# Neighbourhood attention on Trainium2: the position bias added by VectorE on the way out of PSUM, where TensorE had added it with identity products

## The chip, the cores and the metric

The kernel runs on one core of one Trainium2 chip. The metric is the device time of one execution in microseconds. The traces come from one profiled execution; engines are named as in the profile: PE (TensorE's matmuls) and PEld (its weight loads), DVE (VectorE), ACT (ScalarE), POOL (GpSimd), SP (SyncE, whose queue issues every DMA of this kernel).

## The reference

One step of a two-layer network over 1024 latent tokens (a grid of 16 rows of 64) and 128 context tokens of width 1024. Layer 0 mixes pooling and latent attention; layer 1 is 2-D neighbourhood attention with 16 heads of 64. Each layer ends in an MLP. The change lies in the neighbourhood attention of the latent tokens:

```python
s_loc = jnp.einsum('bqhd,bikhd->bhqik', qr, kb, ...) * scale + bias[None]
s_ctx = jnp.einsum('bqhd,blhd->bhql', qr, k_ctx, ...) * scale
s = jnp.concatenate([s_loc.reshape(B, H, GRID_W, kh * GRID_W), s_ctx], axis=-1)
p = jax.nn.softmax(s, axis=-1).astype(v.dtype)
return (jnp.einsum('bhqik,bikhd->bqhd', p_loc, vb)
        + jnp.einsum('bhql,blhd->bqhd', p_ctx, v_ctx))
```

A query sees a window of 8 rows by 16 columns. `bias` is a learned value per head and relative place, and -1e30 outside the window. Context keys have no bias.

## The kernel before, in words

The program is written with a tile library whose scheduler sets the order of the instructions of each engine; semaphores follow from it. Precision is kept by splitting operands into a high and a low half of type fp32r and summing products of halves.

The neighbourhood attention of layer 1 stands near the middle of the program, after the values' projection (`value_gen1`) and before layer 1's output projection and MLP. Tokens are ordered so that eight blocks of 128 keys each touch at most three blocks of 128 queries. A head is a generator, `na_units`, of two context units and eight key tiles:

- `scores` writes the scores of one key tile, 128 keys by 256 or 384 queries, into one of three PSUM banks (`ps_st`, tag `pa`). L1299 multiplies the high and low halves of k (`kk`) with q's high half (`qq`); L1303 multiplies `k2` with q's low half (`q2`), and a row of ones in `k2` with the negated row of maxima in `q2[64:65]`. Between the two, L1302 adds the bias: a product of the identity (`identr`) with the table of the head, once with its high half `tbh` and once with its low half `tbl`. Tiles 1 and 6 of a head take two pieces of the table, the others one: ten pieces and twenty such products a head.
- L1331 takes the exponential from the bank into `p`, and L1336 multiplies `p` with the values `nv` into `ps_pv`. The scores are transposed, keys on partitions, so `p` needs no transpose.
- Context tiles (L1312, L1314) have no bias. Sums and quotients come at the end of a half (L1003, L1004) and of a head pair (L1045 to L1049).

Beside a head, `weave` runs `na_max` for the head two later: eight times two matmuls `ps_m` (L1281, L1282; tag `pb`, three banks), then a VectorE reduction L1284 that adds the table `ta` and takes the maximum. `put_max` turns the result into a row (L1022, L1024), stores it to DRAM (`mrow`), and the load of `q2[64:65]` reads it back. For the first seven heads the context's own attention (`ctxw`, `ps_s`) runs beside them, for the last the output projection (`ps_o`).

`load_na` loads `kk`, `qq` and `ta` two heads ahead, `load_na_rest` loads `k2`, `q2`, `nv` and the table `tb` (128 x 640) one head ahead and splits `tb` with L1266 (ScalarE, `tbh`) and L1267 (VectorE, `tbl`). Most tiles come from 36 slots that are handed out oldest first (`Slots`); `tb`, `q2` and `tbh` come from the weights' rings `wr` (three buffers), `wh` and `wl` (four each). All loads go through SP's queue (L113), in order: a load that waits for a buffer holds up those behind it.

```python
for u, w, c in tabs:
    for t in (th, tlo):
        nc.tensor.matmul(ps[:, u:w], identr, t[:, c:c + w - u], start=False, stop=False)
```

Of the kernel before, what the change touches and what calls it, by code (L numbers as in the profile page):

```python
# [10 lines left out]
F32 = mybir.dt.float32  # L11
F32R = mybir.dt.float32r
AF = mybir.ActivationFunctionType
# [4 lines left out]
P = 128  # L18
# [72 lines left out]
def hybrid_kernel(ctx: ExitStack, tc: tile.TileContext, I, O):  # L91
    nc = tc.nc

    cst = ctx.enter_context(tc.tile_pool(name="cst", bufs=1))
# [5 lines left out]
    S = Slots(spool, NSLOT)  # L100
# [39 lines left out]
    vec = cst.tile([P, NVEC], F32, name="vec")  # L140
    ones = cst.tile([P, P], F32, name="ones")
    ident = cst.tile([P, P], F32, name="ident")
    identr = cst.tile([P, P], F32R, name="identr")
    sel8 = cst.tile([P, 6, 8], F32, name="sel8")
    sel8r = cst.tile([P, 6, 8], F32R, name="sel8r")
    ecnt = cst.tile([P, 4, 16], F32, name="ecnt")
# [7 lines left out]
    def W(tag, name=None):  # L154
        return wpool.tile([P, 1024], F32 if tag == "wr" else F32R, tag=tag, name=name or tag, bufs=3 if tag == "wr" else 4)
# [360 lines left out]
    dma(sel8, I["sel8"])  # L516
    dma(ecnt, I["ecnt"])
    nc.scalar.copy(sel8r, sel8)
    nc.scalar.copy(identr, ident)
    pt = PS("ps_sil", "pb")  # L520
    nc.tensor.transpose(pt[0:16, 0:P], sil, ident)
    sr = S.alloc("sr")
# [20 lines left out]
    for ch in range(NCH):  # L543
        c0 = ch * CH
        for g in range(4):
            ps = PS("ps_i")[:, :CH]
# [72 lines left out]
    for m in (2, 3, 0, 1):  # L619
        w = wtile(wsplit(I["win0"][m]))  # L620
        for ch in range(NCH):
            ps = PS("ps_i")[:, :CH]
# [83 lines left out]
    for ch in range(NCH + 1):  # L706
        cache = ch == NCH
        n = P if cache else CH
        cs = slice(0, P) if cache else slice(ch * CH, ch * CH + CH)
        ps8 = PS("ps8", "pb")[0:8, :n]  # L710
        for t in range(4):
            ps = PS("ps_k")[:, :n]
# [382 lines left out]
    rest = load_rest(0)  # L1095
    opairs = []
    for h in range(8):
# [12 lines left out]
        rest = nrest  # L1110
# [26 lines left out]
    st, h = {}, []  # L1137
# [60 lines left out]
    for g in range(4):  # L1198
# [8 lines left out]
        for t, ch in order:  # L1207
# [3 lines left out]
            ps = PS("ps_n1")[:, :CH]  # L1211
# [9 lines left out]
        for ch in range(NCH):  # L1221
            for t in range(4):
                wn = "naq" if t < 2 else "nak"
                pp_ = pq if t < 2 else pk
                ps = PS("ps_b", "pb")[:, :CH]
# [27 lines left out]
        return kk, qq, ta  # L1253

    def load_na_rest(h):
        k2, q2, v, tb = S.alloc("k2", F32R), W("wh", "q2"), S.alloc("nv"), W("wr", "tb")
        p, n0 = h // 2, 64 * (h % 2)
        rows = slice(n0, n0 + 64)
        dma(k2[0:64], kd[0][p, rows])
        dma(k2[64:65], onesr)  # L1260
        dma(q2[0:64, :NS], qd[1][p, rows])
        dma(q2[64:65, :NS], mrow1[h].rearrange("a b -> (a b)").unsqueeze(0))
        dma(tb[:, :640], I["bias_k"][h])
        load_pv(vd, h, v)
        th, tl = W("wl", "tbh"), S.alloc("tbl", F32R)
        nc.scalar.copy(th[:, :640], tb[:, :640])  # L1266
        nc.vector.tensor_sub(tl[:, :640], tb[:, :640], th[:, :640])  # L1267
        return k2, q2, v, th, tl

    mrow1 = [DR(f"mrow1{i}", [8, P]) for i in range(16)]  # L1270
    od = DR("od", [8, P, TOK], F32)
# [17 lines left out]
        yield  # L1289

    def na_units(h, tl, rest, opair, den):
        (kk, qq, _), (k2, q2, v, th, tlo) = tl, rest
        par = 64 * (h % 2)
        v3 = v.rearrange("p (t f) -> p t f", t=9)
        cp = W("wr", "cp")
        po = [None, None]

        def scores(ps, ks, qs, tabs):
            nc.tensor.matmul(ps, kk[:, ks], qq[:, qs], start=True, stop=False)  # L1299
            for u, w, c in tabs:  # L1300
                for t in (th, tlo):
                    nc.tensor.matmul(ps[:, u:w], identr, t[:, c:c + w - u], start=False, stop=False)  # L1302
            nc.tensor.matmul(ps, k2[0:65, ks], q2[0:65, qs], start=False, stop=True)  # L1303

        def close_half(half):
# [2 lines left out]
        def ctx_unit(half):  # L1308
            qs = slice(half * 512, half * 512 + 512)
            ps = PS("ps_st")  # L1310
            scores(ps, slice(0, P), qs, [])
            nc.scalar.activation(cp[:, qs], ps, AF.Exp)  # L1312
            po[half] = PS("ps_pv", "pc")
            nc.tensor.matmul(po[half], v3[:, 8, :], cp[:, qs], start=True, stop=False)  # L1314
# [4 lines left out]
        for i in range(8):  # L1319
# [6 lines left out]
            n = b - a  # L1326
            p_ = held[:, cnt * CH:cnt * CH + n]
            ps = PS("ps_st")[:, :n]
            tabs = {0: [(0, 256, 128)], 1: [(0, 128, 384), (128, 384, 128)], 6: [(0, 256, 0), (256, 384, 512)]}
            scores(ps, slice(P + i * P, 2 * P + i * P), slice(a, b), tabs.get(i, [(0, n, 0)]))  # L1330
            nc.scalar.activation(p_, ps, AF.Exp)  # L1331
            for half in range(2):
                u, w = max(a, half * 512), min(b, half * 512 + 512)
                if u >= w:
# [77 lines left out]
    for h in range(16):  # L1412
# [23 lines left out]
            of = out_first(1, acts)  # L1436
            gs.append((chain(iter([None] * OW), islice(of, OA)), OW + OA))
        weave(*gs)
        S.free(*tls[h][:2], rest[0], rest[2], rest[4])
        rest = nrest  # L1440
    run(islice(of, OB))
    later(2)
# [148 lines left out]
```

## Time and profile before

| | |
|---|---|
| Time, median of 3 runs | 3052.11 us (3050.89 to 3064.39) |
| Profiled execution: its time, its span | 3059.43 us, 3057.2 us |
| TensorE, matmuls | 2950.9 us busy, 97% |
| TensorE, weight loads | 2663.1 us, 87% |
| VectorE | 2117.4 us, 69% |
| ScalarE | 1337.7 us, 44% |
| GpSimd | 315.5 us, 10% |
| Moved by DMA | 372.39 MB, 122 GB/s on average |

The profiled execution took 7.3 us more than the median; sums over its trace are made against its own 3059.43 us. Matmuls are pipelined, so a row's mean duration of one is longer than the distance from its start to the next one's start. A share of the whole span averages over stages; the stage of the change is read by itself.

### The profile page before, as it was taken

The numbers are of one execution on the slowest core, as the hardware profiler recorded it, in microseconds if no ns is written. First come the engines' busy times: TensorE is split into PE (matmuls) and PEld (weight loads), VectorE is DVE, ScalarE is ACT, GpSimd is POOL, SyncE is SP. The second block draws the span as 40 slices with busy tenths as digits, with TensorE's granted clock in tenths as the row PEclk, the third lists the DMA queues.
The fourth block names the chain that finished last, engine by engine and source line by source line (L and its number), as shares of the span: only waits on it lengthen the run. The fifth ranks groups of instructions, "written<-read, shape, count | busy, mean of one in ns | idle before, by whom it ended". The sixth has DMA issues, their size and how long they took to land.

```text
span 3057.2 us, 46985 instructions
## 1 busy us (share of the span) xinstructions
PE 2950.9 (97%) x18622; PEld 2663.1 (87%) x18622; DVE 2117.4 (69%) x3777; ACT 1337.7 (44%) x2194; POOL 315.5 (10%) x210
## 2 busy tenths in 40 slices
PE   7998999889999999999999999989989999999999
PEld 4956666689999999999988797767989999999999
DVE  5976343797768889786899522544677678777775
ACT  5364344244436544353645422434345355453433
POOL 1014000252000020000221000000021000110000
PEclk9996999999999999999999999999999999999999
DMA  6529331432323334232566346687303232332322
GB/s 233 165 69 312 81 76 50 134 105 83 97 77 96 104 126 146 88 97 84 169 206 208 112 151 176 170 198 204 115 29 93 81 100 73 121 94 87 97 77 87
DMA packets 148269, 372.39 MB, mean 122 GB/s; under 512 B 14225, under 2 KB 67073, under 8 KB 148050
## 3 DMA queue, kind: packets, MB, share of 16 engines
q1 hardware_dynamic: 148050, 369.40, 39.4%
q8 instruction: 146, 2.39, 0.3%
q14 instruction: 73, 0.60, 0.1%
HBM read 310.69 MB, written 57.47 MB: 120 GB/s over the span
## 4 chain that ended last, share of the span: by engine, by line
PE 86%; DVE 5%; DMA 5%; issue 1%; ACT 1%; POOL 1%; SPq 0%; DVEq 0%; ACTq 0%; POOLq 0%
PE ps L453 9%; PE ps L455 9%; PE ps L454 9%; PE ps L423 8%; PE ps L425 7%; PE ps L424 7%; PE ps_pv L1079 4%; PE ps_pv L1336 2%; PE ps_n L336 2%; PE ps_n L337 2%; PE ps_n L338 2%; PE ps_v L1360 1%; DVE trash L201 1%; PE ps_v L1362 1%; PE ps_v L1361 1%
## 5 line engine op out<-in xcount | busy, mean ns | idle before, releaser
L453 PE MATMUL ps<-ml,wh 128*128 128x288 f32 x2048 | 591.9, 295 | 10.1 <-DVE ml L442 7.8
L454 PE MATMUL ps<-mh,wl 128*128 128x288 f32 x2048 | 600.9, 295 | 0.0
L455 PE MATMUL ps<-mh,wh 128*128 128x288 f32 x2048 | 596.5, 295 | 0.0
L423 PE MATMUL ps<-bl,wh 128*128 128x288 f32 x1792 | 532.7, 297 | 13.4 <-DVE bl L354 10.2
L424 PE MATMUL ps<-bh,wl 128*128 128x288 f32 x1792 | 529.5, 295 | 0.0
L425 PE MATMUL ps<-bh,wh 128*128 128x288 f32 x1792 | 528.0, 295 | 0.0
L453 PEld LDWEIGHTS ps<-ml,wh 128*128 128x128 f32 x2048 | 381.3, 188 | 11.1 <-DVE ml L442 8.3
L454 PEld LDWEIGHTS ps<-mh,wl 128*128 128x128 f32 x2048 | 385.2, 188 | 0.0
L455 PEld LDWEIGHTS ps<-mh,wh 128*128 128x128 f32 x2048 | 383.3, 188 | 0.1
L459 DVE SCALAR_TENSOR_TENSOR x<-ps,ada,x 128x288 f32<-128x288 f32 (+2 forms) x640 | 269.8, 450 | 120.3 <-PE ps L455 118.8
L423 PEld LDWEIGHTS ps<-bl,wh 128*128 128x128 f32 x1792 | 336.7, 188 | 16.5 <-issue 11.5
L425 PEld LDWEIGHTS ps<-bh,wh 128*128 128x128 f32 x1792 | 338.3, 189 | 0.0
L424 PEld LDWEIGHTS ps<-bh,wl 128*128 128x128 f32 x1792 | 337.4, 188 | 0.2
L396 ACT CAST wh<-s 128x512 fp32r<-128x512 f32 x256 | 146.1, 618 | 306.9 <-PE ps L455 216.6
L161 ACT CAST wh<-wr 128x1024 fp32r<-128x1024 f32 x188 | 197.0, 1049 | 169.8 <-PE ps L425 80.1
L201 DVE CUSTOM_DVE_ANT_0 trash<-wada,silu 128x1024 bf16<-128x1024 f32 x160 | 214.5, 1340 | 17.9 <-DMA wada<-in_wada 7.6
L162 DVE TENSOR_TENSOR wl<-wr,wh 128x1024 fp32r<-128x1024 f32 x144 | 179.7, 1251 | 44.9 <-ACT wh L161 44.8
L396 ACT CAST wh<-wr 128x1024 fp32r<-128x1024 f32 (+1 forms) x128 | 106.9, 835 | 219.8 <-PE ps L455 155.5
L162 POOL TENSOR_TENSOR wl<-wr,wh 128x1024 fp32r<-128x1024 f32 x44 | 124.1, 2827 | 707.2 <-ACT wh L161 707.1
L1037 DVE TENSOR_REDUCE stat<-ps_m 128x1 f32<-128x384 f32 x192 | 98.3, 551 | 121.2 <-PE ps_m L1036 120.9
L1284 DVE CUSTOM_DVE_ANT_0 trash<-ps_m,ta 128x512 bf16<-128x512 f32 (+1 forms) x128 | 84.0, 656 | 122.0 <-PE ps_m L1282 113.4
L397 DVE TENSOR_TENSOR wl<-s,wh 128x512 fp32r<-128x512 f32 x232 | 157.6, 711 | 5.1 <-ACT wh L396 2.8
(321 smaller groups left out, 6248.9 us busy)
## 6 DMA issues: line engine op xcount, KB each, us to landing
wr<-in_w SPq DMA_DIRECT2D x256, 512.0 KB
wada<-in_wada SPq DMA_DIRECT2D x48, 512.0 KB
wada<-in_wada0t SPq DMA_DIRECT2D x32, 512.0 KB
wr<-in_win SPq DMA_DIRECT2D x24, 512.0 KB
wr<-in_wout SPq DMA_DIRECT2D x24, 512.0 KB
vd<-vst SPq DMA_DIRECT2D x27, 384.0 KB
kk<-kd SPq DMA_DIRECT2D x32, 288.0 KB
nv<-vd SPq DMA_DIRECT2D x16, 576.0 KB
```

The lines of the kernel that those rows point to most:

```text
L161: nc.scalar.copy(hi, r)
L162: (nc.gpsimd if e else nc.vector).tensor_sub(lo, r, hi)
L201: nc.vector.tensor_tensor_reduce(trash, r[:, :D], silu[i][:, :D], scale=1.0, scalar=0.0, op0=ALU.mult, op1=ALU.add, accum_out=a)
L396: nc.scalar.copy(h, src)
L397: (nc.gpsimd if j in EDGE and min(ps) in EDGE_POOL else nc.vector).tensor_sub(l, src, h)
L423: nc.tensor.matmul(ps, wh[:, a], hl[:, b], start=k == 0, stop=False)
L424: nc.tensor.matmul(ps, wl[:, a], hh[:, b], start=False, stop=False)
L425: nc.tensor.matmul(ps, wh[:, a], hh[:, b], start=False, stop=k == 3)
L453: nc.tensor.matmul(ps, wh, hl, start=kk == 0, stop=False)
L454: nc.tensor.matmul(ps, wl, hh, start=False, stop=False)
L455: nc.tensor.matmul(ps, wh, hh, start=False, stop=kk == 3)
L459: nc.vector.scalar_tensor_tensor(x[m][:, a:b], ps[:, a - ch * HC:b - ch * HC], g, x[m][:, a:b], op0=ALU.mult, op1=ALU.add)
```

## The change

`load_na_rest` loads `tb` into the ring `wl` and no longer splits it; `tbh`, `tbl` and `identr` are gone, and with `tbl` one slot per head. `scores` has no products with the identity. After the scores of a key tile, VectorE adds the table's pieces to the bank and writes the sum to `p` in SBUF, and ScalarE takes the exponential of `p` in place.

```diff
 def load_na_rest(h):
-        k2, q2, v, tb = S.alloc("k2", F32R), W("wh", "q2"), S.alloc("nv"), W("wr", "tb")
+        k2, q2, v, tb = S.alloc("k2", F32R), W("wh", "q2"), S.alloc("nv"), W("wl", "tb").bitcast(F32)
...
-        th, tl = W("wl", "tbh"), S.alloc("tbl", F32R)
-        nc.scalar.copy(th[:, :640], tb[:, :640])
-        nc.vector.tensor_sub(tl[:, :640], tb[:, :640], th[:, :640])
-        return k2, q2, v, th, tl
+        return k2, q2, v, tb
...
-        def scores(ps, ks, qs, tabs):
+        def scores(ps, ks, qs):
             nc.tensor.matmul(ps, kk[:, ks], qq[:, qs], start=True, stop=False)
-            for u, w, c in tabs:
-                for t in (th, tlo):
-                    nc.tensor.matmul(ps[:, u:w], identr, t[:, c:c + w - u], start=False, stop=False)
             nc.tensor.matmul(ps, k2[0:65, ks], q2[0:65, qs], start=False, stop=True)
...
-            scores(ps, slice(P + i * P, 2 * P + i * P), slice(a, b), tabs.get(i, [(0, n, 0)]))
-            nc.scalar.activation(p_, ps, AF.Exp)
+            scores(ps, slice(P + i * P, 2 * P + i * P), slice(a, b))
+            for u, w, c in tabs.get(i, [(0, n, 0)]):
+                nc.vector.tensor_add(p_[:, u:w], ps[:, u:w], tb[:, c:c + w - u])
+            nc.scalar.activation(p_, p_, AF.Exp)
...
-        S.free(*tls[h][:2], rest[0], rest[2], rest[4])
+        S.free(*tls[h][:2], rest[0], rest[2])
```

The scheduler makes a new order of it in this stage; up to the stage and from the end of it on, the order is nearly the old one. In the rows below a number behind a name tells allocations apart, and the brackets name the engines or DMA queues that an instruction waits for. The changed kernel's lines are a few lower: L1294 and L1295 are the old L1299 and L1303, L1330 the old L1336, L1306 the old L1314, L1279 the old L1284, L1018 the old L1020, L1324 is the addition.

TensorE at the start of a late head, before:

```order
L1299 MATMUL ps_st<-qq_19321,kk_19320 128x256 [waits PE_49]
L1302 MATMUL ps_st<-tbh,identr 128x256
L1302 MATMUL ps_st<-tbl_19462,identr 128x256
L1303 MATMUL ps_st<-q_19452,k_1356_19451 128x256
L1336 MATMUL ps_pv<-p_19572,nv_19308 128x256 [waits Activation_49]
L1299 MATMUL ps_st<-qq_19321,kk_19320 128x384
L1302 MATMUL ps_st<-tbh,identr 128x128
L1302 MATMUL ps_st<-tbl_19462,identr 128x128
L1302 MATMUL ps_st<-tbh,identr 128x256
L1302 MATMUL ps_st<-tbl_19462,identr 128x256
L1303 MATMUL ps_st<-q_19452,k_1356_19451 128x384
```

and with the change, also from the first key tile (128x256) of a late head:

```order
L1294 MATMUL ps_st<-qq_19452,kk_19451 128x256 [waits DVE_49,PE_49]
L1295 MATMUL ps_st<-q_19577,k_1375_19576 128x256
L1330 MATMUL ps_pv<-p_19690,nv_19443 128x384 [waits Activation_49]
L1294 MATMUL ps_st<-qq_19452,kk_19451 128x384 [waits Activation_49]
L1295 MATMUL ps_st<-q_19577,k_1375_19576 128x384
L1294 MATMUL ps_st<-qq_19452,kk_19451 128x384 [waits DVE_49]
L1295 MATMUL ps_st<-q_19577,k_1375_19576 128x384
L1330 MATMUL ps_pv<-p_19690,nv_19443 128x256 [waits Activation_49]
L1306 MATMUL ps_pv<-cp,nv_19578 128x512 [waits DMAHW1_49,Activation_49]
L1294 MATMUL ps_st<-qq_19452,kk_19451 128x512 [waits DVE_49]
L1295 MATMUL ps_st<-q_19577,k_1375_19576 128x512
L1330 MATMUL ps_pv<-p_19750,nv_19578 128x256 [waits Activation_49]
```

The products with tbh and tbl are gone. The first tile's product of values (the last row) now stands behind the scores of tiles 1 and 2 and of a context unit, and scores wait for VectorE, which empties their bank.

VectorE around the start of a late head (ISA trash,stat is the maximum reduction, ISA stat reads its result out), before:

```order
L1267 TENSOR_TENSOR tbl_19612<-tb,tbh 128x640 [waits DMAHW4_49,Activation_49]
L1020 TENSOR_SCALAR stat<-stat 128x8 [waits DVE_49]
L1284 ISA trash,stat<-ps_m,ta_19617 128x384 [waits DMAHW2_49,PE_49]
L1284 ISA stat 128x1
L1048 SCALAR_TENSOR_TENSOR den_19155<-den_19155,ry_19517 128x1024 [waits Pool_49]
L1284 ISA trash,stat<-ps_m,ta_19617 128x512 [waits DVE_49,PE_49]
L1284 ISA stat 128x1
L1049 SCALAR_TENSOR_TENSOR no_1312_19154<-no_1312_19154,den_19155 128x1024 [waits DVE_49]
L1003 COPY no_1354_19449<-ps_pv 64x512 [waits PE_49]
L1284 ISA trash,stat<-ps_m,ta_19617 128x512 [waits DVE_49,PE_49]
```

and with the change:

```order
L1324 TENSOR_TENSOR p_19610<-ps_st,tb 128x256 [waits DMAHW6_49,PE_49]
L1324 TENSOR_TENSOR p_19610<-ps_st,tb 128x128 [waits PE_49]
L1324 TENSOR_TENSOR p_19610<-ps_st,tb 128x256
L1279 ISA trash,stat<-ps_m,ta_19588 128x384 [waits DMAHW1_49,PE_49]
L1279 ISA stat 128x1
L1279 ISA trash,stat<-ps_m,ta_19588 128x512 [waits DVE_49,PE_49]
L1279 ISA stat 128x1
L1324 TENSOR_TENSOR p_19610<-ps_st,tb 128x384 [waits PE_49]
L1324 TENSOR_TENSOR p_19655<-ps_st,tb 128x384 [waits PE_49,Activation_49]
L1279 ISA trash,stat<-ps_m,ta_19588 128x512 [waits DVE_49,PE_49]
L1279 ISA stat 128x1
```

The additions stand between the maximum reductions of the head two later. The first of a head waits for the load of tb, as the split tbl did before through ScalarE.

SP's queue late in the values' projection, whose results go to DRAM from vst, before, from the load of the first head's tb on (kd and qd are k and q in DRAM, vd the values):

```order
L113 DMA tb<-in_bias_k 128x640 [waits DMAHW2_49,DVE_49]
L113 DMA vd_14388<-vst_17021 128x2x384 [waits DMAHW3_49,Activation_49,Pool_49]
L113 DMA vd_14388<-vst_17081 128x2x384 [waits DMAHW4_49,Activation_49]
L113 DMA k_1132_17833<-kd_14386 64x1152 [waits DMAHW5_49,DMAHW4_49,PE_49]
L113 DMA k_1132_17833<-onesr 1x1152 [waits DMAHW6_49]
L113 DMA vd_14388<-vst_17141 128x2x384 [waits DMAHW7_49,Activation_49]
L113 DMA nv_17835<-vd_14388 128x9x128 [waits DMAHW7_49,DMAHW0_49,PE_49]
L113 DMA vd_14388<-vst_17201 128x2x384 [waits DMAHW1_49,Activation_49]
```

and with the change, the rows up to the first head's tb:

```order
L113 DMA k_1137_17844<-kd_14384 64x1152 [waits DMAHW4_49,DMAHW3_49]
L113 DMA k_1137_17844<-onesr 1x1152 [waits DMAHW5_49]
L113 DMA vd_14386<-vst_17424 128x2x384 [waits Activation_49,Pool_49]
L113 DMA nv_17846<-vd_14386 128x9x128 [waits DMAHW7_49,DMAHW6_49]
L113 DMA vd_14386<-vst_17484 128x2x384 [waits DMAHW0_49,Activation_49]
L113 DMA tb<-in_bias_k 128x640 [waits DMAHW1_49,PE_49]
L113 DMA q_17832<-qd_14383 64x1024 [waits DMAHW2_49,PE_49]
L113 DMA q_17832<-mrow_16670 1x1024
```

The first tb moved from amid the stores of the values to behind the second head's k2 and nv, next to q2, and it waits for TensorE, which still reads the ring wl.

## Rows read from the trace of the kernel before

**Rows 1.** The page: busy time of each engine, its share of the span, instructions.

```profile
PE 2950.9 (97%) x18622; PEld 2663.1 (87%) x18622; DVE 2117.4 (69%) x3777; ACT 1337.7 (44%) x2194; POOL 315.5 (10%) x210
```

**Rows 2.** Busy time by stretch: length, PE, PEld, DVE, ACT, POOL, clock, DMA share, GB/s.

```profile
1864.00:2182.00 318.00, 300.37 (x1425) 225.73 (x1425) 157.04 (x355) 132.55 (x284) 16.57 (x7) 0.95 0.71 189
1864.00:2064.00 200.00, 185.26 (x860) 135.12 (x859) 92.22 (x237) 80.69 (x185) 9.47 (x4) 0.92 0.76 189
2064.00:2182.00 118.00, 115.11 (x565) 90.61 (x566) 64.82 (x119) 51.86 (x100) 7.10 (x3) 0.99 0.62 188
2083.94:2100.64 16.70, 16.70 (x82) 12.48 (x81) 9.96 (x22) 6.73 (x14) 1.30 (x1) 1.00 0.79 231
2182.00:3057.00 875.00, 859.35 (x6366) 857.18 (x6364) 639.12 (x1098) 379.39 (x522) 65.67 (x39) 0.99 0.27 84
```

**Rows 3.** The chain of waits, 1780 to 2260 us: start, length, what.

```profile
1883.71 9.80 DMA tb<-in_bias_k
1893.53 0.72 ACT tbh L1266
...
1951.05 7.05 DMA kk<-kd
...
2011.81 10.00 DMA qq<-qd
...
2053.70 9.20 DMA tb<-in_bias_k
```

**Rows 4.** Busy time by stretch, four microseconds each.

```profile
1868.00:1872.00 4.00, 4.00 (x17) 2.63 (x17) 1.00 (x4) 1.56 (x6) 0.00 (x0) 1.00 0.99 356
2040.00:2044.00 4.00, 0.00 (x0) 0.00 (x0) 1.30 (x3) 2.09 (x4) 0.00 (x0) 0.99 1.04 219
2044.00:2048.00 4.00, 3.98 (x9) 2.76 (x10) 1.32 (x3) 2.39 (x5) 2.36 (x1) 0.59 0.27 61
```

**Rows 5.** Groups by shape, 1864 to 2182 us: busy us, mean ns; idle time ahead.

```profile
L1284 DVE CUSTOM_DVE_ANT_0 trash<-ps_m,ta 128x512 bf16<-128x512 f32 x84 | 57.9, 690 | 33.4 <-PE ps_m L1282 28.6
...
L1331 ACT ACTIVATE p<-ps_st 128x384 f32<-128x384 f32 x96 | 46.7, 490 | 68.5 <-PE ps_st L1303 68.0
...
L1302 PE MATMUL ps_st<-tbl,identr 128*128 128x384 f32 x64 | 23.0, 360 | 0.0
...
L1267 DVE TENSOR_TENSOR tbl<-tb,tbh 128x640 fp32r<-128x640 f32 x14 | 11.5, 824 | 35.2 <-ACT tbh L1266 35.2
...
L1266 ACT CAST tbh<-tb 128x640 fp32r<-128x640 f32 x14 | 10.1, 723 | 33.9 <-DMA tb<-in_bias_k 33.9
```

**Rows 6.** The timeline of TensorE: start, length, engine, line, operation.

```profile
2082.09 0.33 PE L1302 MATMUL ps_st<-tbh,identr 128*128 128x384 f32 x1
...
2082.43 0.34 PE L1303 MATMUL ps_st<-q,k 65*128 65x384 f32 x1
...
2087.29 0.28 PE L1302 MATMUL ps_st<-tbh,identr 128*128 128x256 f32 x1
...
2087.53 0.22 PE L1302 MATMUL ps_st<-tbh,identr 128*128 128x128 f32 x1
...
2087.69 0.39 PE L1303 MATMUL ps_st<-q,k 65*128 65x384 f32 x1
```

**Rows 7.** Line L1302 alone, by stretch: length, PE and PEld busy, clock, DMA.

```profile
1864.00:2064.00 200.00, 40.81 (x190) 33.17 (x190) 0.92 0.76 189
```

**Rows 8.** Waits, 1864 to 2182 us: who for whom, us in total, times, longest.

```profile
ACT tbh L1266 <- DMA tb<-in_bias_k: 33.9, 10, 6.9
...
PE ps_pv L1336 <- ACT p L1331: 7.5, 3, 4.7
```

**Rows 9.** Groups by shape, whole span: VectorE from PSUM, ScalarE from SBUF.

```profile
L436 DVE TENSOR_TENSOR u<-ps,scr 128x288 f32<-128x288 f32 x64 | 28.7, 448 | 2.0 <-PE ps L425 2.0
...
L762 DVE TENSOR_TENSOR kro<-krr,ps_b 128x384 f32<-128x384 f32 x4 | 2.1, 550 | 3.6 <-PE ps_b L685 3.6
...
L325 ACT ACTIVATE sqf<-nr 128x384 f32<-128x384 f32 x48 | 24.9, 519 | 19.3 <-DVE sql L326 17.8 <-PE ps L328 1.1
```

More of the change, by code (lines that the diff above doesn't have):

```diff
@@ L142, in hybrid_kernel @@
     ident = cst.tile([P, P], F32, name="ident")
-    identr = cst.tile([P, P], F32R, name="identr")
     sel8 = cst.tile([P, 6, 8], F32, name="sel8")
@@ L518, in hybrid_kernel @@
     nc.scalar.copy(sel8r, sel8)
-    nc.scalar.copy(identr, ident)
     pt = PS("ps_sil", "pb")
@@ L1291, in na_units @@
     def na_units(h, tl, rest, opair, den):
-        (kk, qq, _), (k2, q2, v, th, tlo) = tl, rest
+        (kk, qq, _), (k2, q2, v, tb) = tl, rest
         par = 64 * (h % 2)
@@ L1310, in ctx_unit @@
             ps = PS("ps_st")
-            scores(ps, slice(0, P), qs, [])
+            scores(ps, slice(0, P), qs)
             nc.scalar.activation(cp[:, qs], ps, AF.Exp)
```

## The prediction

> **What bounds the kernel now.** I read the page first, then the stretches, the chain, the rows by shape and the waits. On the page TensorE is busy 97% of the span [rows 1]; that is an average over stages, so it says only that TensorE is the first suspect. The edit touches one stage, the sixteen heads of neighbourhood attention, which stands between 1864 and 2182 us. There TensorE shows 300.4 of 318 us busy, VectorE 157.0, ScalarE 132.6, and the DMA engines are 0.71 busy [rows 2]. So TensorE sets the pace and nobody else is near it, but its own row hides two things. First, in the early part, 1864 to 2064, it is idle for 200 - 185.3 = 14.7 us and its clock is at 0.92, which is about 0.08 x 200 = 16 us lost; in the rest it is idle for 2.9 us at 0.99. Second, that early part is where the DMA engines are 0.76 busy. The chain of waits shows what the idle time is: it runs through landings of kk, qq and tb, and after tb through ScalarE's cast tbh [rows 3]. The short stretches show how the loss comes about: in 2040 to 2044 TensorE does nothing while the DMA engines are saturated (1.04), and in the next four microseconds the granted clock is at 0.59 [rows 4]. A head in the undisturbed part takes 16.7 us and TensorE is busy in all of it [rows 2].
>
> **The change, part by part.** *Identity products, out.* Sixteen heads x 10 table pieces x 2 halves (tbh, tbl) are 320 matmuls: 128 of 384 columns, 128 of 256, 64 of 128. The row by shape gives 360 ns for one of 384 [rows 5], but matmuls overlap, and the price on TensorE's path is from start to start: two of 384 columns take 2082.09 to 2082.43, so 0.17 us each; two of 256 take 2087.29 to 2087.53, 0.12 each; two of 128 take 2087.53 to 2087.69, 0.08 each [rows 6]. The sum is 128 x 0.17 + 128 x 0.12 + 64 x 0.08 = 21.8 + 15.4 + 5.1 = 42.3 us, or 2.6 us of a head's 16.7. The early part holds 190 of the 320 [rows 7], so 25.1 us of it falls there and 17.2 us later.
>
> The Trainium skill (TensorE: Matmul & The Clock Gate, Wait — 56ns, not 53.3ns?) gives N / 2.4 GHz + 2.5 ns between starts. By that the removed products would be worth an estimated 128 x 162.5 + 128 x 109.2 + 64 x 55.8 ns = 38.4 us; the rows are 4 us above it, because the short ones do not come closer than 0.08 us here, and I keep the rows.
>
> *Table split, out.* Sixteen casts tbh on ScalarE (723 ns) and sixteen subtractions tbl on VectorE (824 ns) go [rows 5]; 11.6 and 13.2 us on engines with room. I cost them at nothing. What may count is that ScalarE no longer stands 33.9 us in ten waits for tb ahead of its exponentials [rows 8]. The cast of ident at the start of the program is one instruction beside a load: nothing.
>
> *Additions, in.* Each of the 128 score tiles gets a VectorE addition out of PSUM, two for tiles 1 and 6 of a head: 64 of 384 columns, 64 of 256, 32 of 128. None exists before; the nearest rows are the same instruction on other tiles, 550 ns at 384 columns and 448 at 288 [rows 9]. The slope, 1.06 ns a column, gives 414 and 278 ns for 256 and 128. That is 64 x 0.550 + 64 x 0.414 + 32 x 0.278 = 35.2 + 26.5 + 8.9 = 70.6 us. VectorE's stage goes from 157.0 - 11.5 to 216 us: 73% of a stage of 295 us, so it stays under TensorE, whose dense need, without the 17.6 us idle and the 17 us of slow clock, falls to 318 - 17.6 - 17 - 42 = 241 us. But an addition now stands between the scores and the exponential, in VectorE's one queue, behind maximum reductions of 0.69 us [rows 5]. If all of that were exposed, the 70.6 us would lie on the path and the stage would be 28 us longer; if the three score banks hide it, it is free. The order shows a product of values two or three tiles behind its scores, so I take it near free: 4 us of the 17.2 in the later part is given back, mostly at the start of a head and in the last 40 us, where VectorE has the output projection's splits too.
>
> *Exponential.* It reads p in SBUF in place of the bank. An activation of 384 columns from SBUF takes 519 ns [rows 9] against 490 [rows 5]: 128 x 0.03 = 4 us on an engine that is 42% busy. Nothing. The bank is now freed by VectorE, one step sooner than the exponential would.
>
> *Loads.* tb's loads are the same sixteen, but they take a buffer of the weights' ring wl. The values' projection holds that ring until its last products, so the first two tb, which were issued amid its stores, now stand behind k2, nv and the last stores, next to q2. That adds 2 x 328 KB to a stretch that moves 356 GB/s and is full (0.99) [rows 4]: 1.8 us if it shows, nothing if q2's row of maxima is later anyway. I take 1 us. Later loads keep their number and size, and each head takes one slot less, so a slot comes free earlier.
>
> *What the early part gives back.* It moves 0.76 x 200 = 152 us of DMA work. Shortened by all of 25.1 us it would be 0.87 busy, in bursts that already saturate. Nothing of the 25.1 us is gained if the loads set the pace of these heads; all of it, and some of the 14.7 + 16 us, if the waits are only the queue's late issue. The chain has six landings in these nine and a half heads [rows 3], so neither end is plainly the nearer; I take half, 12.5 us.
>
> **Sum** against the profiled execution, 3059.4 us: 12.5 + 17.2 - 4 - 1 = 24.7, so about 3035 us. The runs' median lies 7.3 us under that execution, so the forecast is 3052.1 - 25 = **3027 us**, 0.8% faster. A measurement of this kernel can tell about 0.5%, 15 us, from no change.
>
> **Rivals.**
> 1. *The loads come earlier and the whole of it shows.* For it: a slot per head comes free, so SP's queue can run further ahead; ScalarE's stand for tb goes. Against: the DMA engines are at 1.04 where TensorE idles. It gives 42.3 plus half of 14.7 + 16, 57 us: 2995 us, between 2988 and 3012.
> 2. *The loads pace the early heads.* For it: 0.76 busy on average and full in every gap. Then the early part keeps its 200 us and only 17.2 - 4 - 1 = 12 us is left: 3040 us, no change that can be told, between 3037 and 3056.
> 3. *VectorE stands for tb (the slower side).* The first addition of a head waits for tb in VectorE's queue, and behind it stand the maximum reductions that free the other three banks and feed the row of maxima, for which SP's queue waits before it issues more loads. ScalarE's 33.9 us of waits [rows 8] would be VectorE's. If they reach TensorE, each idle microsecond costs 1 + 16 / 14.7 = 2.09 with its clock: 33.9 x 2.09 - 42.3 = +29 us, 3081 us. It decides from 42.3 / 2.09 = 20 us of such idle time on. Against: the cast was placed ahead of the head, the addition comes only after its first scores, so the same landing is late less often; and of the 33.9 us little reached TensorE (its products waited 7.5 us for p [rows 8]).
> 4. *The clock falls without a long gap.* TensorE would stop briefly at each bank that VectorE holds, and be granted less throughout. With 0.75 on average its 241 us would become 321, and with 17.6 us idle the stage 339: +21, 3073 us. The rows speak against it: in the last MLP, where every bank is emptied by VectorE, the clock is at 0.99 [rows 2].
>
> The Trainium skill (TensorE: Matmul & The Clock Gate, A second HAM failure mode: psum-queue depth-cycling) tells of a kernel in which small stops between groups made the clock swing. By that rule the time would be rival 4's, and the trace so far does not bear it out.
>
> That the change might not do what it says is no case here: the built order has no product with the identity left in this stage and 160 additions.
>
> **How the numbers follow.** Forecast 0.45 (own range 3013 to 3037), rival 1 0.20, rival 2 0.23, rival 3 0.09, rival 4 0.03. Faster by over 0.5%, under 3037: forecast and rival 1, 0.65. Within 0.5%: rival 2, 0.23. Slower: rivals 3 and 4, 0.12. The range leaves out these last and a third of rival 1, 0.06, so 0.18: from 2992 to 3056, which also holds both ends of the early part's unknown.
>
> **What would show it.** The heads' stage should last some 293 us in place of 318; an undisturbed head 14 to 15 us; VectorE's additions 550, 414 and 278 ns and its stage near 216 us; TensorE waiting for p and for score banks by a few microseconds; idle gaps still behind kk, qq or tb with the DMA engines full, and the clock low only after them. The first MLP and the last should stand as before. The prediction is wrong if an undisturbed head stays over 16 us (the additions are on the path), if VectorE's waits for tb sum to over 20 us with TensorE idle beside them (rival 3), if the early part stays at 200 us (rival 2), or if the stage is under 270 us (rival 1).

## The result, and the profile after

The changed kernel takes **3025.84 us** (median of 4 runs, 3023.98 to 3030.89) where the kernel before takes 3052.75 (4 runs beside them); the ratio is 0.9916, with a 95% interval of 0.9892 to 0.994. The forecast was 3027. That the number fits is luck in part: two terms of the working were off by some 20 us each, in opposite directions, and the experiments below are about those two.

The profiled execution took 3023.98 us. Its page, busy time by engine, against [rows 1]:

```profile
PE 2910.4 (96%) x18302; PEld 2611.2 (86%) x18302; DVE 2160.5 (71%) x3921; ACT 1330.5 (44%) x2177; POOL 312.7 (10%) x210
```

The 320 products are gone, 160 additions have come. The next rows are stretches of the heads' stage (length; PE, PEld, DVE, ACT, POOL busy; clock; DMA share; GB/s). They run from the first head's first exponential on and are cut where head 11 begins, first for the kernel before, then for the change.

```profile
1865.30:2091.20 225.90, 210.94 (x976) 154.24 (x976) 106.02 (x269) 92.39 (x207) 11.85 (x5) 0.92 0.73 184
2091.20:2181.00 89.80, 87.13 (x436) 69.61 (x437) 50.40 (x86) 38.64 (x73) 4.72 (x2) 1.00 0.65 202
```

```profile
1858.40:2045.20 186.80, 177.34 (x748) 116.78 (x749) 131.22 (x359) 87.15 (x194) 11.84 (x5) 0.95 0.92 225
2045.20:2145.00 99.80, 85.89 (x343) 60.08 (x343) 68.20 (x140) 38.21 (x72) 4.74 (x2) 0.90 0.56 168
```

Read them against each other and the odd thing stands out. The first eleven heads gained 39 us, though the products that left them were priced at about 29. The remaining heads *lost* 10 us, though some 13 us of products left them too: 14 us idle where there were 3, and a clock of 0.90 where it was 1.00. (About 7 us of the difference between the two profiled executions lie ahead of the stage, in code that did not change; the one before was 7 us above its median.)

The groups by shape of the stage, 1857.3 to 2145 us (busy us, mean ns; idle time ahead and what ended it):

```profile
L1324 DVE TENSOR_TENSOR p<-ps_st,tb 128x384 f32<-128x384 f32 x64 | 35.1, 554 | 25.4 <-PE ps_st L1295 25.0
L1324 DVE TENSOR_TENSOR p<-ps_st,tb 128x256 f32<-128x256 f32 x63 | 26.4, 418 | 17.9 <-PE ps_st L1295 17.6
...
L1324 DVE TENSOR_TENSOR p<-ps_st,tb 128x128 f32<-128x128 f32 x32 | 9.1, 284 | 1.9 <-PE ps_st L1295 1.7
```

```profile
L1325 ACT ACTIVATE p<-p 128x384 f32<-128x384 f32 x96 | 49.3, 522 | 66.1 <-DVE p L1324 65.7
```

An addition costs 554, 418 or 284 ns, 70.6 us in all, and an exponential from SBUF 522 ns against 490 [rows 5]: the prices were right. The waits of the same stretch (who for whom, us in total, times, longest), against [rows 8]:

```profile
ACT p L1325 <- DVE p L1324: 77.4, 66, 4.6
...
DVE p L1324 <- PE ps_st L1295: 44.3, 45, 6.9
...
PE ps_st L1295 <- DMA q<-mrow: 13.9, 5, 7.1
...
PE ps_st L1294 <- DVE p L1324: 3.9, 5, 1.7
```

ScalarE's 33.9 us of standing for tb have gone and no wait of VectorE for tb has come in their place. TensorE waits 3.9 us for a score bank that VectorE holds. But a wait is there that the stage before did not list: 13.9 us in which the second score product stands for q2, whose last row holds the maxima and comes through DRAM (mrow).

The longest of these, 7.1 us at the start of head 12, can be followed through three timelines (start, length, engine, line, operation). ScalarE has the row ready at 2048.20:

```profile
2048.20 0.24 ACT L1022 CAST row<-ps_mt 8x128 fp32r<-8x128 f32 x1
```

SP, whose queue issues every DMA, comes to its write eight microseconds later, after loads of the next heads that stand for their slots and for earlier transfers, and to the load of the row only when the write has landed:

```profile
2048.60 0.45 SPq L113 DMA_DIRECT2D k<-kd  x1
2051.66 0.24 SPq L113 DMA_DIRECT2D k<-onesr  x1
2054.33 0.34 SPq L113 DMA_DIRECT2D ta<-in_bias_q  x1
2055.25 0.61 SPq L113 DMA_DIRECT2D kk<-kd  x1
2056.31 0.29 SPq L113 DMA_DIRECT2D mrow<-row  x1
...
2062.98 0.24 SPq L113 DMA_DIRECT2D q<-mrow  x1
```

And TensorE goes on 4.0 us after that:

```profile
2066.98 1.30 PE L1295 MATMUL ps_st<-q,k 65*128 65x512 f32 x3 [7.11 <-DMA q<-mrow]
```

The stop costs more than its own length. Behind it the granted clock is 0.50 for 20 us, the lower of its two levels (1.2 GHz), so that 17 busy us did the work of 8 or 9:

```profile
2064.00:2084.00 20.00, 17.02 (x38) 10.31 (x38) 9.01 (x22) 6.91 (x13) 2.37 (x1) 0.50 0.33 79
```

### The profile page after: what moved, and what is told of

The parts are those of the page before. It is cut to its first block, busy times and chain, and to the rows that moved or that the text cites. A ratio compares the mean times of both kernels' runs of the same rounds, so it can differ in the third digit from the quotient of the medians.

```text
span 3022.2 us, 46490 instructions
## 1 busy us (share of the span) xinstructions
PE 2910.4 (96%) x18302; PEld 2611.2 (86%) x18302; DVE 2160.5 (71%) x3921; ACT 1330.5 (44%) x2177; POOL 312.7 (10%) x210
## 4 chain that ended last, share of the span: by engine, by line
PE 84%; DVE 6%; DMA 6%; issue 2%; ACT 1%; POOL 1%; SPq 0%; DVEq 0%; POOLq 0%; ACTq 0%
PE ps L452 9%; PE ps L454 9%; PE ps L453 9%; PE ps L422 8%; PE ps L424 8%; PE ps L423 8%; PE ps_pv L1077 4%; PE ps_n L335 2%; PE ps_n L336 2%; PE ps_n L337 2%; DVE trash L200 1%; PE ps_pv L1330 1%; PE ps_v L1354 1%; PE ps_v L1356 1%; PE ps_v L1355 1%
## 5 line engine op out<-in xcount | busy, mean ns | idle before, releaser
L1279 DVE CUSTOM_DVE_ANT_0 trash<-ps_m,ta 128x512 bf16<-128x512 f32 (+1 forms) x128 | 83.5, 652 | 98.1 <-PE ps_m L1277 90.4
```

## The experiments

Two questions. Where did the 39 us of the first eleven heads come from, if the products are only a part? And what do the additions cost late, if not VectorE's time? All kernels ran beside the kernel before, whose medians were 3052.66 to 3054.34 us from batch to batch, so the times below may be set side by side; the runs of one kernel spread over 4 to 14 us (16 for E6, 30 for E9), so steps under 5 us are not told apart. Besides the time I give, from one trace each, the length of the first eleven heads (first exponential of head 0 to that of head 11; the expectations call this stretch twelve heads) and of the next four (head 11 to head 15). The trace is of one execution, whose own time can lie at an end of its kernel's spread: 3028.44 us for E6, 3032.83 for E7, 3016.09 for E8, 3012.53 for E12.

| kernel | median us (lowest to highest) | ratio, 95% interval | heads 0 to 11 | 11 to 15 |
|---|---|---|---|---|
| before | 3052.75 (3050.89 to 3064.39) | 1 | 225.9 | 63.2 |
| the change | 3025.84 (3023.98 to 3030.89) | 0.9916 [0.9892, 0.994] | 186.8 | 76.7 |
| E1 before, no products | 3026.30 (3022.35 to 3029.76) | 0.991 [0.989, 0.9929] | 209.5 | 53.1 |
| E2 change, no additions | 3003.93 (2996.55 to 3005.15) | 0.9829 [0.9805, 0.9854] | 191.0 | 53.6 |
| E3 change, split kept | 3042.10 (3035.90 to 3043.35) | 0.9961 [0.9943, 0.9979] | 208.0 | 67.4 |
| E4 last heads on TensorE | 3024.36 (3022.76 to 3026.79) | 0.9904 [0.9886, 0.9922] | 187.7 | 68.1 |
| E5 table on ring wr | 3021.28 (3013.54 to 3024.70) | 0.9887 [0.9859, 0.9914] | 190.5 | 64.5 |
| E6 slot held | 3038.30 (3028.44 to 3044.59) | 0.9939 [0.9921, 0.9957] | 202.0 | 65.6 |
| E7 split of a landed table | 3026.30 (3025.94 to 3032.83) | 0.9914 [0.9894, 0.9935] | 200.4 | 64.3 |
| E8 one table | 3022.62 (3016.09 to 3029.78) | 0.9898 [0.9869, 0.9927] | 181.9 | 71.4 |
| E9 split kept, no slot | 3044.37 (3032.47 to 3062.20) | 0.9974 [0.9956, 0.9993] | 204.5 | 77.4 |
| E10 oh on ScalarE | 3024.98 (3023.24 to 3033.24) | 0.9909 [0.9887, 0.9931] | 191.0 | 75.8 |
| E11 row of ones | 3006.05 (3001.91 to 3010.92) | 0.984 [0.9816, 0.9865] | 184.8 | 53.6 |
| E12 row on GpSimd | 3010.86 (3003.57 to 3012.53) | 0.9846 [0.9831, 0.9862] | 195.0 | 55.7 |

### E1, E2, E3: the change taken apart

E1 is the kernel before without the identity products, and nothing in their place:

```diff
-            for u, w, c in tabs:
-                for t in (th, tlo):
-                    nc.tensor.matmul(ps[:, u:w], identr, t[:, c:c + w - u], start=False, stop=False)
```

> The kernel before without the 320 identity products and without additions; the table is still loaded and split, on ring wr and with its slot. The position bias is left out. Theory (TensorE's products were the price of the early heads, and VectorE's queue gives part back late): some 50 us faster than before, about 3000 us; first context unit of head 0 to that of head 11 about 187 us in place of 225.9, the rest of the stage about 76 in place of 89.6. Rival A (the early gain came from ScalarE and VectorE no longer standing for tb and from the slot set free): the split still stands here, so the early heads gain little, under 15 us, and the time stays over 3030 us.

E2 is the change without the additions:

```diff
-            for u, w, c in tabs.get(i, [(0, n, 0)]):
-                nc.vector.tensor_add(p_[:, u:w], ps[:, u:w], tb[:, c:c + w - u])
-            nc.scalar.activation(p_, p_, AF.Exp)
+            nc.scalar.activation(p_, ps, AF.Exp)
```

> The changed kernel without the 160 additions; the exponential reads the bank again, tb is still loaded. The position bias is left out. Theory: the early heads, where the DMA engines are 0.92 busy, stay at 187 us within 4; the late part falls from 99.6 us to about 77, since VectorE was 0.93 busy there; about 3003 us. Rival B (the late part lost by the late row of maxima and full DMA engines, not by VectorE): the late part stays over 93 us and the time over 3018 us.

E3 is the change with the split of the table as before (its results unused), tb back on the ring wr and the slot for the low half held:

```diff
+        th, tl = W("wl", "tbh"), S.alloc("tbl", F32R)
+        nc.scalar.copy(th[:, :640], tb[:, :640])
+        nc.vector.tensor_sub(tl[:, :640], tb[:, :640], th[:, :640])
```

> The changed kernel with the table still cast by ScalarE and split by VectorE, tb back on ring wr and the slot held; nothing reads the two halves. Theory: VectorE has 13 us and ScalarE 12 us more, mostly beside other work: 3026 to 3034 us, early heads 187 to 193 us. Rival A: ScalarE and VectorE stand for tb as before, so the early heads lose 10 us or more, 197 us and over, and the time is 3036 us or more.

These three with the two kernels make the change a sum of three steps, and two of the steps can be taken in either order:

- products out: 3052.7 to 3026.3, **-26.4 us** (before to E1);
- split, slot and ring out: **-22.4** without additions (E1 to E2), **-16.3** with them (E3 to the change);
- additions in: **+21.9** without the split (E2 to the change), **+15.8** with it (E1 to E3).

E1 missed its forecast by 26 us, and that is the finding: what I had taken for free, the split, holds the early heads back. Rival A had this reason; of its numbers (under 15 us early, over 3030 us) 16.4 and 3026.3 came. E3 went to its rival A, E2 to its theory in the time. The table's columns say where each step lies. With the split, the first eleven heads take 208 to 210 us, with additions or without; without it 187 to 191. And the four late heads take 53 us in both kernels without additions. The additions cost nothing early and, without the split, 23 us late.

The waits of E3 over its first heads (1859 to 2067 us) show the standing that is back:

```profile
ACT tbh L1264 <- DMA tb<-in_bias_k: 30.7, 10, 6.1
...
PEld ps_pv L1333 <- ACT p L1328: 17.1, 8, 4.4
DVE tbl L1265 <- ACT tbh L1264: 16.3, 5, 5.3
```

Cast and subtraction wait for a table that has not landed, and behind them stand the exponentials that TensorE's products of values need. TensorE's own wait for them, 0.7 us in the change over the whole stage, is in E3 over these heads:

```profile
PE ps_pv L1333 <- ACT p L1328: 14.5, 5, 4.2
```

The stretches of E1 and of E2 show what it does to TensorE, without additions:

```profile
1860.70:2070.20 209.50, 193.88 (x755) 127.00 (x756) 103.42 (x265) 91.98 (x208) 11.81 (x5) 0.85 0.83 196
```

```profile
1858.60:2049.60 191.00, 179.65 (x753) 119.87 (x754) 92.84 (x254) 86.76 (x197) 11.82 (x5) 0.91 0.85 204
```

The same number of products takes 14 us longer in E1, at a granted clock of 0.85 against 0.91, and the idle time is 4 us more. So most of the early loss is clock: 0.15 of 209.5 us against 0.09 of 191 are 31 and 17 us. One stretch of E1 holds over half of its 31. TensorE stops for 2.5 us at 1885.8, waiting for p; then it is busy without a break, and its granted clock is 0.50 for 37.5 us:

```profile
1888.90:1926.40 37.50, 37.50 (x95) 23.92 (x93) 16.09 (x43) 12.41 (x30) 2.35 (x1) 0.50 0.55 133
```

### E4: the last heads back on TensorE

Heads 13 to 15 get their bias by identity products as before, the others by additions:

```diff
+        if not (h >= 13):
+            return k2, q2, v, tb
+        th, tl = W("wl", "tbh"), S.alloc("tbl", F32R)
...
+            here = tabs.get(i, [(0, n, 0)])
+            scores(ps, slice(P + i * P, 2 * P + i * P), slice(a, b), here if split else ())
```

> The changed kernel with heads 13 to 15 alone on identity products (their tables are split again), heads 0 to 12 on additions. Theory: VectorE loses 3 x 4.4 us of additions and takes 3 x 0.8 us of splits in the part where it is the bound, TensorE takes 3 x 2.6 us where it stands idle: 6 to 11 us faster than the change, 3015 to 3020 us, all of it after head 11. Rival B: no gain, 3024 us or more.

3024.36 us, within the spread of the change: no gain that can be told. In its trace heads 11 to 15 are 8.6 us shorter, but from head 0's first exponential to the end the two traces are only 3.4 us apart, and TensorE still stands 2.9 us for the row of head 15. So it is not enough to take additions away from the last three heads; the late loss has another handle (E11, E12).

### E5 to E7, E9: what of the split it was

The split brought a ring, a slot, work on two engines, and the standing for the table. E5 moves only the ring:

```diff
-        k2, q2, v, tb = S.alloc("k2", F32R), W("wh", "q2"), S.alloc("nv"), W("wl", "tb").bitcast(F32)
+        k2, q2, v, tb = S.alloc("k2", F32R), W("wh", "q2"), S.alloc("nv"), W("wr", "tb")
```

> The changed kernel with the tables loaded into the ring wr (three buffers, shared with cp) instead of wl (four, otherwise unused here). Keeping the split of the table cost 16 to 22 us in the runs before this one. Theory (the cost is ScalarE's and VectorE's standing for a table that hasn't landed, 37.2 and 19.8 us of waits in the run with the split kept): the ring is worth nothing, 3023 to 3029 us, twelve heads in 184 to 191 us. Rival (the wr ring holds back the tables' loads): 3036 to 3043 us, twelve heads in 203 to 210 us.

E6 holds only the slot:

```diff
+        tl = S.alloc("tbl", F32R)
+        return k2, q2, v, tb, tl
```

> The changed kernel with one more slot of the pool held by each head, as the table's low half held it, and nothing written into it. Theory (standing for the table): 3023 to 3029 us, twelve heads in 184 to 191 us. Rival (one slot fewer in the rotation makes kk, qq, k2 and the values wait for their slots and land later): 3034 to 3043 us, twelve heads in 200 to 210 us.

E7 is E3 with the split reading a table that landed long ago:

```diff
-        nc.scalar.copy(th[:, :640], tb[:, :640])
-        nc.vector.tensor_sub(tl[:, :640], tb[:, :640], th[:, :640])
+        if h == 0:
+            kept.append(S.alloc("tbk"))
+            dma(kept[0][:, :640], I["bias_k"][h])
+        nc.scalar.copy(th[:, :640], kept[0][:, :640])
+        nc.vector.tensor_sub(tl[:, :640], kept[0][:, :640], th[:, :640])
```

> The run with the split kept, in which the cast and the subtraction read a table that was loaded once, with head 0, and has long landed; each head's own table is still loaded into wr and read by the additions, and the low half's slot is still held. So the split's work (0.83 us of ScalarE and 0.72 us of VectorE for each head) stays, and only the standing for the table goes. Theory (standing): 3025 to 3032 us, twelve heads in 186 to 194 us. Rival (the work, the ring and the slot cost it): 3037 to 3043 us, twelve heads in 203 to 210 us.

E9 is E3 with the low half in the ring wl, so that no slot is held:

```diff
-        th, tl = W("wl", "tbh"), S.alloc("tbl", F32R)
+        th, tl = W("wl", "tbh"), W("wl", "tbl")
```

> The run with the split kept, with the low half written into the ring wl (beside the high half) instead of a slot of the pool: the cast, the subtraction and their standing for the table stay, the held slot goes. So far: neither 3023 to 3031 us, a slot held alone 3028 to 3045, slot with standing 3036 to 3043, slot with the work but without standing 3026 to 3033. Theory (standing for the table is what costs): 3036 to 3043 us, twelve heads in 200 to 210 us. Rival (the slot is what costs, and the run of the landed table was quick for another reason, its other rotation of the slots): 3022 to 3030 us, twelve heads in 185 to 193 us.

The ring is worth nothing that can be told (E5). E7 does all of the work, holds the slot and takes what the change takes (the cast is ScalarE's, 0.73 us, and the subtraction VectorE's, 0.82; the expectation has them the other way round). **Work and standing without the slot cost about 18 us** (E9, 3044.37). By these two totals it is the standing that costs. Its waits in E9, 1863 to 2068 us:

```profile
ACT tbh L1264 <- DMA tb<-in_bias_k: 40.4, 11, 9.0
...
DVE tbl L1265 <- ACT tbh L1264: 19.9, 6, 6.3
```

So E9 goes to the theory, and E6 to its rival: a slot held and never written took 3038.30 us, 12 more than the change, though two of its seven runs (3028.44 and 3030.14) lie within the change's spread. E6 and E7, which both hold the slot, have 200 to 202 us for their first eleven heads, between the two groups. E7's time is that of the change and within its theory, but its first eleven heads missed the 186 to 194 us of that theory: they are 13.6 us longer than the change's, and the next four 12.4 shorter. So the equal totals of E7 and the change are sums of unequal parts, and the standing is the best account of the split's price but not the whole of it. The two causes do not add up either: E3 with both takes no longer than E9 with one. In E6 SP's queue stands longer for the maxima's write than in the change. SP's waits over the stage, the change and E6:

```profile
SPq L113 <- DMA mrow<-row: 16.4, 10, 3.4
```

```profile
SPq L113 <- DMA mrow<-row: 43.1, 12, 6.6
```

E7 shows 37.9 us on that row and is not slower, and E2, the quickest of all, 44.7; so this row does not settle it. What a slot is worth, apart from the order in which slots come round, stays open.

### E8: do the loads pace the early heads?

One table is loaded, with head 0, and read by all:

```diff
-        dma(tb[:, :640], I["bias_k"][h])
+        if h == 0:
+            kept.append(S.alloc("tbk"))
+            dma(kept[0][:, :640], I["bias_k"][h])
+        tb = kept[0]
```

> The changed kernel with one table, loaded with head 0 and read by every head's additions: 15 loads of 327,680 B, 4.9 MB, are left out (and each head but the first gets another head's bias). Theory that the first twelve heads go at the pace of their loads (DMA 0.92 busy at 225 GB/s there): twelve of the left-out loads at 225 GB/s are 17.5 us, so 3005 to 3012 us, twelve heads in 167 to 173 us. Rival (the loads are not what paces them, but the order in which the engines serve two heads): 3019 to 3027 us, twelve heads in 182 to 188 us.

3022.62 us, and 181.9 us for the first eleven heads where 167 to 173 would have shown a pace set by bytes. The four runs lie in two pairs, near 3016 and near 3029, and even the first pair, with the trace, stays above the theory. So the rival holds: a DMA share of 0.92 was not the limit here, since leaving 4.9 MB of loads out gave 10 us at the most and 3 in the median. One thing speaks for the theory and was not tried by itself: E8's table stays in a slot of the pool for the whole stage, which may have cost some of the gain (E6).

### E10, E11, E12: why additions cost time late

E10 takes seven casts of 0.76 us out of VectorE's late queue:

```diff
-            nc.vector.tensor_copy(a[0], o)
+            nc.scalar.copy(a[0], o)
```

> The changed kernel with the casts of the output projection's operands (oh, 0.756 us, seven of them in the last four heads' 100 us) on ScalarE instead of VectorE. Theory (the late part grew by 16 to 22 us because the additions stand in VectorE's queue behind its long instructions): 5.3 us of VectorE less late, so 3018 to 3023 us and the late part 4 to 6 us shorter. Rival (VectorE isn't the bound, the chain scores, addition, exp, product is, and ScalarE's exps now stand behind casts that wait for their data): 3025 to 3033 us.

3024.98 us and 75.8 us for the late heads: nothing gained; the time is at the lower edge of the rival's range. E2's expectation had VectorE 0.93 busy late; over the change's late stretch it is 68.2 of 99.8 us, and 0.92 only in 28 us near its end (2103 to 2131). That VectorE's time is not what the late heads lost is shown better by E11, which keeps all of VectorE's work.

E11 takes away the standing for the maxima:

```diff
-NA_SCALE = 0.125
+NA_SCALE = 0.0078125
...
-        dma(q2[64:65, :NS], mrow1[h].rearrange("a b -> (a b)").unsqueeze(0))
+        dma(q2[64:65, :NS], onesr[:, :NS])
```

> The changed kernel with the row of q2 that carries the maxima loaded from a row of ones (and the scores' scale divided by 16, so that the exp stays in range): the maxima are still computed and written out, but no head's scores stand for them; the attention's values are other ones. Theory (the additions cost time late because the maxima, which share VectorE with them, come later, and TensorE stands for the row: 13.9 us of waits for q<-mrow, in two waits of 6.7 and 3.9 on the chain that ended last): 3008 to 3016 us. Rival (the additions' own link between scores and exp costs it, whatever the row): 3022 to 3030 us.

3006.05 us, 20 less than the change, a little below the range that the theory gave. The early heads stay as they were (184.8 against 186.8 us) and the late ones fall from 76.7 to 53.6, the length that they have without additions. So by the times 20 of the additions' 22 us are paid at one place, where TensorE stands for the row. The trace is less clean: behind head 15's first exponential E11 takes 9 us more than the change (38.3 against 29.2 us to the last product of values), where the chain that ended last runs through VectorE's queue (2100 to 2115 us).

E12 keeps the row and every value, and changes only who issues its two small DMAs (the page lists GpSimd's as a queue and kind of its own, software_dynamic, 1024 packets):

```diff
-        dma(d, r[0:8, 0:P])
+        (nc.sync if dst is not None else nc.gpsimd).dma_start(d.bitcast(F32), r[0:8, 0:P].bitcast(F32))
...
-        dma(q2[64:65, :NS], mrow1[h].rearrange("a b -> (a b)").unsqueeze(0))
+        nc.gpsimd.dma_start(q2[64:65, :NS].bitcast(F32), mrow1[h].rearrange("a b -> (a b)").unsqueeze(0).bitcast(F32))
```

> The changed kernel with two small DMAs of each head issued by GpSimd, which has next to nothing else in this stage, instead of SP: the write of the row of maxima and its load into q2. In the changed kernel's trace the row of head 12 is ready at 2048.2 us, its write is issued at 2056.3 behind other loads on SP's queue and lands at 2063.0, its load is issued then, and TensorE goes on at 2067; without any standing for the row the time was 3006 us. Theory (SP's queue ahead of the two DMAs is what makes the row late): 3008 to 3018 us, and the waits of scores for q<-mrow below 5 us in all. Rival (the landing times of the two DMAs among the stage's other transfers, 6.7 and 3.9 us, make it late, whichever engine issues them): 3022 to 3030 us.

**3010.86 us**, 15 less than the change and 43 less than the kernel before (0.9846, 0.9831 to 0.9862): the best of the kernels that compute everything. The late heads take 55.7 us. Timelines of E12, ScalarE and then GpSimd: the row of head 12 is ready at 2050.52, its write goes out 0.55 us later instead of 8.1, and its load 10 us before that head begins at 2068.67.

```profile
2050.52 0.26 ACT L1022 CAST row<-ps_mt 8x128 fp32r<-8x128 f32 x1 [0.24 <-PE ps_mt L1020]
```

```profile
2051.07 0.52 POOL L1023 DMA_DIRECT2D mrow<-row  x1 [5.43 <-ACT row L1022]
2058.13 0.52 POOL L1260 DMA_DIRECT2D q<-mrow  x1 [6.54 <-PE ps_pv L1330]
```

TensorE's wait for the row is down from 13.9 us to:

```profile
PE ps_st L1295 <- DMA q<-mrow: 2.0, 1, 2.0
```

and the late stretch, 2055 to 2133 us, is 78 us long with a clock of 1.00, against 99.8 and 0.90:

```profile
2055.00:2133.00 78.00, 75.17 (x332) 54.24 (x333) 65.78 (x133) 37.26 (x69) 8.51 (x9) 1.00 0.70 206
```

Between write and load lie 7.1 us here and 6.7 in the change, so what got shorter is the queue ahead of the write, not the way through DRAM. The edit also frees SP from standing for the row itself: in the change SP waits 13.7 us for the row's cast and 16.4 for its write to land, and the loads behind wait with it. How much of the 15 us is that, no run separates. In this trace the gain lies late (21 us), and the first eleven heads are 8 us longer than in the change; one trace of each can't tell whether that is more than the spread. The Trainium skill (DMA: Bandwidth & Descriptors, Issuing engines are not separate DMA queues) says that issuing on several engines saves only the time in which the issuing engine initiates the DMA, usually small beside the transfer. No row here bears on its other half, that all transfers run on the same DMA engines. But what a second queue saved here was the time that a small, urgent DMA stood behind waiting ones, 8.1 us for head 12's write alone, and with 15.0 us in all it was not small.

## Why the prediction was right, and where it was not

*Products out, 42.3 us, of which the early part keeps half of its share.* The mechanism held. E1 measures -26.4 us. In the traces 10.1 us lie in the four late heads, where four times the 2.6 us per head are 10.6, and 16.4 us in the first eleven, where I had allowed 12.5 for the early part and 4.0 for the 30 products between its end and head 11. That the products' price shows whole in dense heads and about half in heads that wait for loads was the right reading of [rows 2] and [rows 6]. Only the half itself was a guess between two ends, and one remark was wrong: of the 4 us between the 42.3 and the 38.4 us set beside it, the short products make up 1.5.

*Table split, costed at nothing: the step that failed.* It was worth 16 to 22 us. I had read the row, ScalarE's 33.9 us of standing for tb [rows 8], and set it aside because TensorE's products waited only 7.5 us for p by name. That was the error: a stop of ScalarE's queue reaches TensorE under other names too, and as a lower clock behind the stop. In E1 TensorE waits 6.2 us for p and 6.0 for another instruction of ScalarE (ctxw), and it has 0.85 of the clock and 14 us more of busy time than E2 for the same number of products. I had put a price on this, 2.09 us for each idle one, but only in rival 3. How the price divides between standing and slot stays open (E6, E7). Rival 1 had the mechanism among its reasons, with a gain of 57 us in all; without additions it came to 48.8 (E2).

*Additions, near free, 4 us given back: the second step that failed.* Their length was right within 6 ns (550, 414 and 278 forecast). They cost 16 to 22 us. My test for exposure was whether three score banks hide an addition, and they nearly do: 3.9 us of waits for a bank. What I did not follow was the path of the maxima's row through ScalarE's cast, SP's queue, DRAM and back. With the additions in, that row arrives after the head's first product could start. With it off SP's queue, the change is 6.9 us above the kernel without additions (E12 against E2), near the 4 us that I had put down. The time from cast to write is 36.5 us over all heads in the change and 32.5 in E2, so SP's standing was there without additions too. For head 12 both parts can be read: in E2 the row is cast 17.9 us ahead of the head's first exponential and its load issued 10.7 us after the cast; in the change TensorE has run out of other work 11.7 us after the cast (2059.87), and the load is issued 14.8 us after it. So with additions the slack shrank by about 6 us and the way grew by 4. By my own sign (an undisturbed head over 16 us means that the additions are on the path) the late heads, at 19.2 us, said so.

*Loads.* The ring, costed at 1 us: E5 can't tell it from nothing. Rival 2, loads that set the early pace: E8 speaks against it, within what its slot leaves open.

*Rivals 3 and 4.* VectorE has no listed wait for tb, so the slower side did not come; the placing of the addition behind a head's first scores was the reason given, and it held. In the change the clock fell only behind stops of TensorE: around the wait for head 12's row TensorE is busy 2.89 us of ten, and in the next ten the granted clock is 0.50.

```profile
2057.00:2067.00 10.00, 2.89 (x15) 1.79 (x13) 2.89 (x9) 0.58 (x1) 0.00 (x0) 0.85 1.03 226
2067.00:2077.00 10.00, 10.00 (x25) 6.40 (x26) 4.62 (x12) 5.58 (x10) 2.37 (x1) 0.50 0.35 91
```

*The sum.* -24.7 was forecast and -26.9 came, out of -26.4, about -19 and about +19 where I had put -29.7 (with the early half), 0 and +4 (and 1 for the ring). It came out right because two errors of like size had opposite signs, and that was luck. The total could not show it, and the stage as a whole hardly (29 us shorter, 286.6 against 315.7, where 25 were forecast); the stage cut in two did, with eleven heads at 17.0 us each on average where the late ones, forecast as the dense part at 14 to 15, took 19.2 from head 11 to head 15.

## What to carry to other kernels

When an operation goes, ask what its engine stood for, not only how long it ran: an instruction that waits at the head of an engine's queue holds up what stands behind it, and taking the split with its standing away was worth as much here (16 to 22 us) as the 160 additions cost. When an operation comes onto a path, follow every result that shares its engine to the next engine that needs it, small DMAs included, and look at what is queued ahead of them. A small, urgent transfer does not belong on a queue of large loads that wait for their buffers.

## What the hardware showed that I had not expected

- A DMA share of 0.92 over 187 us at 225 GB/s was not what set the pace: 4.9 MB of loads less gave 3 us in the median, 10 in its quickest run, where 17.5 were forecast for the early heads alone (E8).
- Behind a stop of 2.5 us the granted clock was 0.50 for 37.5 us, though TensorE was busy in all of them (E1).
- Two 4 KB DMAs a head, moved from SP to GpSimd, gave 15.0 us, and GpSimd's issue took 0.52 to 0.70 us each.
- A slot of the pool held without being written cost 12 us in the median of one kernel (E6), and another that held it too took no longer than the change (E7); the rows don't say why.
